# A plain first pair in every feed-forward stage, and weight sums made by accumulating DMAs

## The chip, the cores and the metric

One core of a Trainium2 chip runs the whole program. The time is the device time of one execution in microseconds (us). The engines are TensorE (PE in the profile, PEld for its weight loads), VectorE (DVE), ScalarE (ACT), GpSimd (POOL) and SyncE (SP), which issues the DMAs of the kernel before.

## What is computed

Two layers of an encoder on 512 tokens of 1024 channels, in float32. Each layer is a half-weighted feed-forward stage, a mixer (a gated spatial unit and a bidirectional mLSTM, with one input and one output projection), and a second half-weighted feed-forward stage; a root-mean-square norm stands ahead of each and at the end. Cut to the part that the change touches:

```python
def rms_norm(x, g):
    return x * lax.rsqrt(jnp.mean(x * x, axis=-1, keepdims=True) + EPS) * g

def swiglu(x, w_gate, w_up, w_down):
    return (jax.nn.silu(x @ w_gate) * (x @ w_up)) @ w_down

for l in range(DEPTH):
    h = x + 0.5 * swiglu(rms_norm(x, ffn1_norm[l]), ffn1_w_gate[l], ffn1_w_up[l], ffn1_w_down[l])
    h = h + mixer(rms_norm(h, mix_norm[l]))
    x = h + 0.5 * swiglu(rms_norm(h, ffn2_norm[l]), ffn2_w_gate[l], ffn2_w_up[l], ffn2_w_down[l])
return rms_norm(x, final_norm)
```

The hidden width of a feed-forward stage is 2816, which is 22 blocks of 128.

## The kernel before

Everything is kept transposed: 128 channels on the partitions, tokens along the row. A float32 operand is used as two rounded halves, hi and lo: ScalarE makes hi by a cast, VectorE makes lo by a subtraction, and each product is three matmuls (hi by hi, hi by lo, lo by hi) that accumulate in PSUM. The norm's gain is multiplied into the activations and its reciprocal root is multiplied into the result, so a product can begin before the statistics are known.

**Pairs.** There are four feed-forward stages. In each, the 22 hidden blocks of gate and up are made in 11 pairs (q = 0 to 10) of two blocks, in groups of 4, 4 and 3 pairs; behind each group stand 8 down products (line 206 to 208 on `pd`), which add to x. One pair computes gate and up for two blocks. As a two by two block product it is done in seven products by Strassen's method, in the form with shared sums (`strassen_pair`): the weights of the pair lie in DRAM as four blocks b11, b12, b22, b21 of 128x1024 (512 KB each), and the seven weight operands are b11, b12 - b11, b22 - that, b22, b12 - b22, b21 and b21 - the second sum. `pair_plan` makes them: four loads by SyncE and four subtractions on VectorE (`combine`, line 149), each followed by `halves` (cast at line 144, subtraction at line 145). The operands of the activations are A11, A12, A22 and four sums S1 to S4, for each of four pairs of channel blocks (j). `Wide.split` makes all seven as x comes in: A11, A12 and A22 are cast and split at lines 367 and 368, the four sums are formed at line 369 into `fb` and cast and split at lines 374 and 375. Each of the seven products is 24 matmuls of 256 columns (lines 159 to 161).

**The first stage's first pair** is done without Strassen, because x and the weights come in piece by piece: 16 products per j, from A11, A12, A22 and A21, of three matmuls of 256 columns each (lines 1060 to 1062), in four PSUM banks. `gated_plain` finishes it, with a reciprocal root over the full width (`rstd`, lines 325 to 341). In the other three stages the first pair is a Strassen pair with `opening` set: its first three products run over j = 0 to 2 together before they take j = 3, and the statistics come from `rstd_tok` and its `spread` within this pair.

**Buffers and order.** `take` hands out the weight operands in the order of the plan and has AHEAD of them made in advance (4 in a feed-forward stage). Halves alternate between two buffers of the phase (`whix`, `wlox`) and three shared ones (`whi`, `wlo`); down and mixer weights use the shared ones alone. Raw blocks alternate likewise between `rawx` (3) and `raw` (3). The framework's scheduler orders each engine's instructions at compile time by their place in the program and by when it expects their inputs and buffers; `issue_after` and `keep_in_program_order` pin a few.

Of the kernel before, what the change touches and what calls it, by code (L numbers as in the profile page):

```python
# [8 lines left out]
F32 = mybir.dt.float32  # L9
# [25 lines left out]
class Net:  # L35
    AHEAD = {"X": 4, "M": 2, "F": 2}
# [17 lines left out]
    def masks(self):  # L54
# [4 lines left out]
        make_identity(nc, self.ident)  # L59
        self.tri = []  # L60
# [63 lines left out]
    def rawx(self):  # L124
        self.turn += 1
        if self.turn % 2:
            return self.phase.tile([P, 1024], F32, tag="rawx", name="rawx", bufs=3)
        return self.wp.tile([P, 1024], F32, tag="raw", name="raw")

    def load(self, src):  # L130
        raw = self.rawx()
        self.nc.sync.dma_start(out=raw, in_=src.rearrange("p j i c -> p (j i c)"))
        return raw

# [47 lines left out]
    def load_parts(self):  # L182
        self.wturn = getattr(self, "wturn", 0) + 1
        raw = self.rawx()
# [156 lines left out]
A11, A12, A22, S3, S1, S2, S4 = range(7)  # L341


class Wide(Norm):
    def __init__(self, b, g):
        super().__init__(b, g)
        self.d = 0
        self.eng = b.nc.vector
        self.spread = None

    def split(self, x):
# [5 lines left out]
        if d % 2 == 0:  # L357
            self.fa = b.wide("fa").rearrange("p (q t) -> p q t", q=4)
            for q in (1, 0):
                nc.scalar.mul(self.fa[:, q, :], x[:, (1 - q) * 256:(2 - q) * 256], g)  # L360
            return
        fa = self.fa
# [3 lines left out]
        fb = b.wide("fb").rearrange("p (q t) -> p q t", q=4)  # L366
# [10 lines left out]
        self.last = fa  # L377
# [87 lines left out]
def strassen_pair(b, norm, rstd, opening):  # L465
# [3 lines left out]
    three = ((pa, A11), (pe, S1), (pb, S2))  # L469
    if opening:  # L470
        ws = [b.take() for _ in three]
        for js in (range(3), (3,)):
            for (p, idx), w in zip(three, ws):
                b.strassen(p, w, X, idx, True, js)
    else:
        for p, idx in three:
            b.strassen(p, b.take(), X, idx, True)
# [6 lines left out]
    spread = None  # L484
    if rstd is None:
        rstd, _, spread = norm.rstd_tok()
    b.strassen(pb, b.take(), X, S3, False)
    U = b.wide("U").rearrange("p (t i c) -> p t i c", t=2, i=2)
# [3 lines left out]
    nc.vector.tensor_tensor(out=U[:, 1], in0=q(pb), in1=q(e5), op=ALU.add)  # L492
    nc.vector.tensor_tensor(out=U[:, 0], in0=q(pe), in1=q(u2), op=ALU.add)
    b.strassen(pa, b.take(), X, A12, False)
    if spread is not None:
        spread()
# [6 lines left out]
    return halved(b, G, True), rstd  # L503


def pair_plan(blocks):
    st = {}

    def e0(b):
        st["b11"] = b.load(blocks[0])  # L510
        return b.halves(st["b11"])

    def e1(b):
        st["b12"] = b.load(blocks[1])
        b.combine(st["b11"], st["b12"], st["b11"])
        return b.halves(st["b11"])

    def e2(b):
# [653 lines left out]
```

## Time and profile before

| | |
|---|---|
| median of 3 runs | 1793.61 us (1792.57 to 1794.6) |
| the profiled execution | 1797.66 us |
| its span, first to last instruction | 1795.9 us |
| TensorE busy | 1759.7 us, 98% |
| VectorE busy | 1396.1 us, 78% |
| ScalarE busy | 868.7 us, 48% |
| GpSimd busy | 98.6 us, 5% |
| DMA moved | 173.60 MB, 97 GB/s on average |

The profile is one execution. The engines run side by side, so the shares do not add up. TensorE's matmuls overlap in their records, so its busy time is longer than the work at its pitch; how many matmuls of which width lie in a stretch tells more. The granted clock is the share of TensorE's full 2.4 GHz, 0.5 being 1.2 GHz. A wait is put down to what came last before it ended.

### The profile page before, as it was taken

How to read it: one execution, taken by the hardware profiler on the slowest of the kernel's cores; microseconds unless marked ns; L12 is line 12 of the kernel's file. 1: busy time of each engine (PE TensorE's matmuls, PEld its weight loads, DVE VectorE, ACT ScalarE, POOL GpSimd, SP SyncE). 2: the span in 40 equal slices, each digit the busy share in tenths (PEclk: the TensorE clock that was granted, in tenths of full speed). 3: DMA queues.
4: the chain of work that ended last, by engine and by line, in shares of the span. 5: the costliest groups of instructions: out<-in, count | busy, mean ns of one | idle time of the engine just before them, and what ended most of it. 6: DMA issues, size and time to landing. Idle time of an engine off the chain costs nothing.

```text
span 1795.9 us, 28343 instructions
## 1 busy us (share of the span) xinstructions
PE 1759.7 (98%) x11626; PEld 1610.3 (90%) x11626; DVE 1396.1 (78%) x2113; ACT 868.7 (48%) x1223; POOL 98.6 (5%) x164
## 2 busy tenths in 40 slices
PE   8999999999998999999989999999999999999998
PEld 8889989887888989989889899898888799899898
DVE  8967958667988957958889588595698989597685
ACT  7434424557555524525545244254576545254255
POOL 6100000103010000000010000002030000000000
PEclk9999999999998999999999999999999999999999
DMA  5332322321241333323323223223112224233223
GB/s 188 95 129 87 122 86 80 97 82 47 66 146 59 114 110 95 118 82 93 108 95 118 82 90 124 89 75 106 59 60 83 91 86 129 84 105 118 83 77 109
DMA packets 51394, 173.60 MB, mean 97 GB/s; under 512 B 5824, under 2 KB 7872, under 8 KB 51264
## 3 DMA queue, kind: packets, MB, share of 16 engines
q1 hardware_dynamic: 51264, 171.79, 29.9%
q8 instruction: 91, 1.49, 0.3%
q14 instruction: 39, 0.32, 0.1%
HBM read 169.67 MB, written 2.10 MB: 96 GB/s over the span
## 4 chain that ended last, share of the span: by engine, by line
PE 85%; DVE 9%; ACT 3%; issue 1%; DMA 1%; SPq 0%; POOL 0%; DVEq 0%; ACTq 0%; POOLq 0%
PE pd L206 9%; PE pd L208 9%; PE pd L207 9%; PE pb L159 6%; PE pb L160 6%; PE pb L161 6%; PE pe L160 4%; PE pa L159 4%; PE pa L160 4%; PE pe L159 4%; PE pa L161 4%; PE pe L161 4%; PE pm L206 3%; PE pm L207 3%; PE pm L208 3%
## 5 line engine op out<-in xcount | busy, mean ns | idle before, releaser
L179 ACT CAST whi<-raw 128x1024 fp32r<-128x1024 f32 (+2 forms) x157 | 151.9, 967 | 317.9 <-PE pd L207 157.5
L206 PE MATMUL pd<-hh,whi 128*128 128x512 f32 (+1 forms) x752 | 282.9, 377 | 0.4 <-ACT hh L448 0.4
L207 PE MATMUL pd<-hl,whi 128*128 128x512 f32 (+1 forms) x752 | 282.6, 376 | 0.6 <-DVE hl L449 0.6
L208 PE MATMUL pd<-hh,wlo 128*128 128x512 f32 (+1 forms) x752 | 282.6, 376 | 0.5 <-DVE wlo L180 0.5
L180 DVE TENSOR_TENSOR wlo<-raw,whi 128x1024 fp32r<-128x1024 f32 (+2 forms) x157 | 176.4, 1125 | 30.0 <-ACT whi L179 29.1
L598 DVE SCALAR_TENSOR_TENSOR x<-pd,x 128x512 f32<-128x512 f32 x88 | 60.7, 690 | 152.1 <-PE pd L208 152.0
L206 PEld LDWEIGHTS pd<-hh,whi 128*128 128x128 f32 x752 | 141.4, 188 | 29.5 <-ACT hh L448 4.3
L208 PEld LDWEIGHTS pd<-hh,wlo 128*128 128x128 f32 x752 | 141.6, 188 | 26.0 <-DVE wlo L180 0.8
L207 PEld LDWEIGHTS pd<-hl,whi 128*128 128x128 f32 x752 | 141.6, 188 | 26.0 <-DVE hl L449 0.8
L144 ACT CAST whi<-rawx 128x1024 fp32r<-128x1024 f32 x86 | 88.6, 1048 | 150.1 <-DVE rawx L149 92.0
L159 PE MATMUL pb<-xh,whix 128*128 128x256 f32 x528 | 153.2, 290 | 4.3 <-ACT u L482 3.4
L161 PE MATMUL pb<-xh,wlox 128*128 128x256 f32 x528 | 151.3, 287 | 0.6 <-DVE wlox L145 0.6
L160 PE MATMUL pb<-xl,whix 128*128 128x256 f32 x528 | 151.3, 286 | 0.0
L144 ACT CAST whix<-rawx 128x1024 fp32r<-128x1024 f32 x86 | 89.8, 1049 | 114.8 <-PE pb L160 80.1
L159 PE MATMUL pb<-xh,whi 128*128 128x256 f32 x504 | 142.2, 282 | 0.1
L160 PE MATMUL pb<-xl,whi 128*128 128x256 f32 x504 | 142.1, 282 | 0.0
L161 PE MATMUL pb<-xh,wlo 128*128 128x256 f32 x504 | 141.5, 281 | 0.5 <-DVE wlo L145 0.5
L144 ACT CAST whi<-raw 128x1024 fp32r<-128x1024 f32 x64 | 67.1, 1048 | 103.0 <-issue 40.5
L145 DVE TENSOR_TENSOR wlo<-rawx,whi 128x1024 fp32r<-128x1024 f32 x86 | 105.1, 1222 | 9.2 <-ACT whi L144 8.9
L145 DVE TENSOR_TENSOR wlox<-rawx,whix 128x1024 fp32r<-128x1024 f32 x86 | 105.0, 1221 | 9.1 <-ACT whix L144 9.1
L159 PEld LDWEIGHTS pb<-xh,whix 128*128 128x128 f32 x528 | 103.0, 195 | 5.8 <-ACT u L482 4.2
L159 PE MATMUL pe<-xh,whi 128*128 128x256 f32 x352 | 101.9, 290 | 5.4 <-ACT xh L374 5.4
(331 smaller groups left out, 5065.7 us busy)
## 6 DMA issues: line engine op xcount, KB each, us to landing
rawx<-in_wst SPq DMA_DIRECT2D x86, 512.0 KB, 3.6
raw<-in_wst SPq DMA_DIRECT2D x86, 512.0 KB, 3.6
raw<-in_wd SPq DMA_DIRECT2D x64, 512.0 KB, 3.6
raw<-in_wd SPq DMA_DIRECT2D x37, 384.0 KB, 3.1
raw<-in_win SPq DMA_DIRECT2D x24, 512.0 KB, 3.5
raw<-in_wo SPq DMA_DIRECT2D x16, 512.0 KB, 3.5
raw<-in_wv SPq DMA_DIRECT2D x8, 512.0 KB, 3.5
x<-in_xT SPq DMA_DIRECT2D x8, 256.0 KB, 4.0
```

The lines of the kernel that those rows point to most:

```text
L144: self.copied = nc.scalar.copy(hi, raw)
L145: nc.vector.tensor_tensor(out=lo, in0=raw, in1=hi.bitcast(F32), op=ALU.subtract)
L159: nc.tensor.matmul(o, whi[:, j, i, :], hi, start=f, stop=False, skip_group_check=True)
L160: nc.tensor.matmul(o, whi[:, j, i, :], lo, start=False, stop=False, skip_group_check=True)
L161: nc.tensor.matmul(o, wlo[:, j, i, :], hi, start=False, stop=j == 3, skip_group_check=True)
L179: self.copied = nc.scalar.copy(hi[:, r], raw[:, r])
L180: nc.vector.tensor_tensor(out=lo[:, r], in0=raw[:, r], in1=hi[:, r].bitcast(F32), op=ALU.subtract)
L206: nc.tensor.matmul(ps, whi[:, k0 + k, :], xh, start=k == 0, stop=False)
L207: nc.tensor.matmul(ps, whi[:, k0 + k, :], xl, start=False, stop=False)
L208: nc.tensor.matmul(ps, wlo[:, k0 + k, :], xh, start=False, stop=k == n - 1)
L598: nc.vector.scalar_tensor_tensor(out=xd, in0=pd, scalar=0.5, in1=xd, op0=ALU.mult, op1=ALU.add)
```

## The change

- Every feed-forward stage begins with a plain pair (`plain_plan`, `plain_step`), as the first stage did. Three Strassen pairs become plain ones.
- `Wide.split` makes A11, A12, A22 and A21 (hi and lo) only. `Wide.sums` makes the four sums for all j, in place, behind the plain pair's matmuls in the program; two of them with the opposite sign. The statistics come from `rstd_tok` behind it in all four stages. `spread` and `gated_plain` for the plain pair stand behind the first product (A11) of the second pair.
- The weight operands of a Strassen pair are made as running sums: p = b11, + b12, + b22, + b21 in one `rawx` tile, q = b22, + b12 in a `raw` tile, r = b21 in another. Each addition is a DMA issued by GpSimd that accumulates into the tile (`add`). The signs that differ are put right in the activations' sums and in two instructions of the pair's end, which become `scalar_tensor_tensor`. The `opening` form of the pair is gone.
- AHEAD in these stages is 5, the constants are made in two parts (`eye` earlier), and the ring for GpSimd's DMAs is 2048.

```diff
-    AHEAD = {"X": 4, "M": 2, "F": 2}
+    AHEAD = {"X": 5, "M": 2, "F": 2}
...
+    def add(self, raw, src):
+        self.nc.gpsimd.dma_start(out=raw, in_=src.rearrange("p j i c -> p (j i c)"), accum_op=ALU.add)
...
-    def combine(self, out, a, c):
-        self.nc.vector.tensor_tensor(out=out, in0=a, in1=c, op=ALU.subtract)
...
-A11, A12, A22, S3, S1, S2, S4 = range(7)
+A11, A12, A22, S3, S2, S4, S1 = range(7)
...
         nc.scalar.copy(hi[:, 0:3], fa[:, 1:4])
+        nc.scalar.copy(a21[:, 0], fa[:, 0])
         nc.vector.tensor_tensor(out=lo[:, 0:3], in0=fa[:, 1:4], in1=hi[:, 0:3].bitcast(F32), op=ALU.subtract)
-        sub = lambda o, a, c, op=ALU.subtract: nc.vector.tensor_tensor(out=fb[:, o - S3], in0=a, in1=c, op=op)
-        sub(S1, fa[:, 0], fa[:, 3], ALU.add)
-        sub(S2, fb[:, S1 - S3], fa[:, 1])
-        sub(S4, fa[:, 2], fb[:, S2 - S3])
-        sub(S3, fa[:, 1], fa[:, 0])
-        nc.scalar.copy(hi[:, 3:7], fb)
-        nc.vector.tensor_tensor(out=lo[:, 3:7], in0=fb, in1=hi[:, 3:7].bitcast(F32), op=ALU.subtract)
+        nc.vector.tensor_tensor(out=a21[:, 1], in0=fa[:, 0], in1=a21[:, 0].bitcast(F32), op=ALU.subtract)
...
+    def sums(self):
+        nc = self.b.nc
+        for fa, (hi, lo) in zip(self.fas, self.xs):
+            f = lambda i: fa[:, i - S3]
+            nc.vector.tensor_tensor(out=f(S1), in0=f(S1), in1=f(S3), op=ALU.subtract)
+            nc.vector.tensor_tensor(out=f(S3), in0=f(S2), in1=f(S3), op=ALU.subtract)
+            for o, a, m in ((S2, f(S1), f(S2)), (S4, f(S4), f(S2))):
+                nc.vector.scalar_tensor_tensor(out=f(o), in0=a, scalar=-1.0, in1=m, op0=ALU.mult, op1=ALU.subtract)
+            nc.scalar.copy(hi[:, 3:7], fa)
+            nc.vector.tensor_tensor(out=lo[:, 3:7], in0=fa, in1=hi[:, 3:7].bitcast(F32), op=ALU.subtract)
...
+    def whole(name, src, chain):
+        def make(b):
+            st[name] = b.load(src, chain)
+            return b.halves(st[name])
+        return make
+
+    def more(name, src):
+        def make(b):
+            b.add(st[name], src)
+            return b.halves(st[name])
+        return make
+
+    return [whole("p", b11, True), more("p", b12), more("p", b22), whole("q", b22, False), more("q", b12),
+            whole("r", b21, False), more("p", b21)]
+
+
+def plain_plan(blocks):
+    def whole(k):
+        return lambda b: b.halves(b.load(blocks[k], k % 2 == 0))
+    return [whole(k) for k in range(4)]
...
+            if q == 0:
+                banks = first
+                if banks is None:
+                    blocks = [b.take() for _ in range(4)]
+                    banks = plain_banks(b)
+                    for j in range(4):
+                        plain_step(b, norm, j, blocks, banks)
+                norm.sums()
+                rstd["full"], _, spread = norm.rstd_tok()
+
+                def between():
+                    spread()
+                    hs.extend(gated_plain(b, *banks, rstd["full"]))
+
                 continue
-            h, rstd = strassen_pair(b, norm, rstd, q == 0)
-            hs += h
+            hs.extend(strassen_pair(b, norm, lambda: rstd["full"], between if q == 1 else None))
```

## Rows read from the trace of the kernel before

**Rows 1.** The page's first lines: span, busy time and instructions of TensorE.

```profile
span 1795.9 us, 28343 instructions
PE 1759.7 (98%) x11626; PEld 1610.3 (90%) x11626; DVE 1396.1 (78%) x2113; ACT 868.7 (48%) x1223; POOL 98.6 (5%) x164
```

**Rows 2.** Windows: stretch, length, busy us (x instructions), PEclk, DMA share, GB/s.

```profile
40.00:80.00 40.00, 34.17 (x251) 32.89 (x251) 36.94 (x38) 17.86 (x21) 11.05 (x22) 0.91 0.30 89
180.00:200.00 20.00, 20.00 (x171) 20.00 (x170) 18.90 (x20) 9.55 (x11) 0.00 (x0) 1.00 0.33 95
240.00:260.00 20.00, 20.00 (x90) 16.58 (x89) 7.67 (x8) 4.10 (x4) 0.00 (x0) 1.00 0.32 99
545.00:581.00 36.00, 30.69 (x209) 28.73 (x208) 31.22 (x52) 17.44 (x25) 0.00 (x0) 0.86 0.19 60
901.00:937.00 36.00, 31.35 (x226) 29.41 (x225) 30.72 (x51) 15.93 (x20) 6.93 (x19) 0.91 0.35 108
1428.00:1464.00 36.00, 30.67 (x207) 28.77 (x206) 30.66 (x50) 17.04 (x25) 0.00 (x0) 0.86 0.20 59
```

**Rows 3.** TensorE's waits in 540:580: us, times, longest.

```profile
PE pe L159 <- ACT xh L374: 2.6, 2, 2.0
PE pe L160 <- DVE xl L375: 0.9, 1, 0.9
PE pa L160 <- DVE xl L368: 0.9, 1, 0.9
PE pa L159 <- ACT xh L367: 0.9, 1, 0.9
```

**Rows 4.** VectorE's groups of instructions in 525:575: count, busy us, mean ns, idle.

```profile
L979 DVE TENSOR_TENSOR x<-pm,x 128x512 f32<-128x512 f32 x8 | 5.4, 682 | 0.6 <-PE pm L208 0.6
L375 DVE TENSOR_TENSOR xl<-fb,xh 128x1024 fp32r<-128x1024 f32 x4 | 4.9, 1220 | 0.0
L368 DVE TENSOR_TENSOR xl<-fa,xh 128x768 fp32r<-128x768 f32 x4 | 3.8, 949 | 0.0
L369 DVE TENSOR_TENSOR fb<-fa 128x256 f32<-128x256 f32 x8 | 3.3, 434 | 0.0
```

**Rows 5.** ScalarE's timeline, 160:171: start, us, instruction, idle before and releaser.

```profile
160.51 1.05 ACT L144 CAST whix<-rawx 128x1024 fp32r<-128x1024 f32 x1 [0.58 <-PE pe L160]
164.17 2.00 ACT L144 CAST whi<-rawx 128x1024 fp32r<-128x1024 f32 x2 [2.61 <-DVE rawx L149]
169.99 1.05 ACT L144 CAST whix<-rawx 128x1024 fp32r<-128x1024 f32 x1
```

**Rows 6.** TensorE's timeline: first matmul of three successive products of one pair.

```profile
168.91 0.28 PE L159 MATMUL pa<-xh,whix 128*128 128x256 f32 x1
171.78 0.28 PE L159 MATMUL pe<-xh,whi 128*128 128x256 f32 x1
...
174.61 0.28 PE L159 MATMUL pb<-xh,whix 128*128 128x256 f32 x1
```

**Rows 7.** VectorE's timeline, 161:171: the split of a block, and a sum of blocks.

```profile
161.59 1.23 DVE L145 TENSOR_TENSOR wlox<-rawx,whix 128x1024 fp32r<-128x1024 f32 x1 [0.26 <-ACT whix L144]
162.85 1.22 DVE L149 TENSOR_TENSOR rawx<-raw,rawx 128x1024 f32<-128x1024 f32 x1
```

**Rows 8.** The page's DMA issues: count, KB each, median us from issue to landing.

```profile
rawx<-in_wst SPq DMA_DIRECT2D x86, 512.0 KB, 3.6
...
raw<-in_wd SPq DMA_DIRECT2D x37, 384.0 KB, 3.1
```

**Rows 9.** GpSimd's timeline, 0:100: two equal products of the parameters.

```profile
33.96 1.30 POOL L660 TENSOR_TENSOR rv<-rv,ct 128x64 f32<-128x64 f32 x1
...
39.14 0.32 POOL L660 TENSOR_TENSOR rv<-rv,ct 128x64 f32<-128x64 f32 x1
```

**Rows 10.** The chain's long pieces, and TensorE's timeline where one product starts within another.

```profile
39.02 3.27 DVE rstd L336
...
82.54 0.28 PE L160 MATMUL pa<-xl,whix 128*128 128x256 f32 x1
82.66 0.39 PE L159 MATMUL pb<-xh,whi 128*128 128x256 f32 x1
```

More of the change, by code (lines that the diff above doesn't have):

```diff
@@ L122, in take, with load @@
         return self.ready.pop(0)
[L124 to L131, printed above, removed]
+    def load(self, src, chain=False):
+        raw = (self.phase.tile([P, 1024], F32, tag="rawx", name="rawx", bufs=3) if chain else
+               self.wp.tile([P, 1024], F32, tag="raw", name="raw"))
         self.nc.sync.dma_start(out=raw, in_=src.rearrange("p j i c -> p (j i c)"))
         return raw
+    def add(self, raw, src):
+        self.nc.gpsimd.dma_start(out=raw, in_=src.rearrange("p j i c -> p (j i c)"), accum_op=ALU.add)
     def halves(self, raw):
@@ L462, in gated_plain, with plain_banks, plain_step, strassen_pair @@
     return halved(b, g)
-def strassen_pair(b, norm, rstd, opening):
+def plain_banks(b):
+    return [b.bank("mm", "pm") for _ in range(2)], [b.bank("sm", "pm") for _ in range(2)]
+def plain_step(b, norm, j, blocks, banks):
+    nc = b.nc
+    pg, pu = banks
+    hi, lo = norm.xs[j]
+    for k, out, second in ((0, pg, False), (1, pu, False), (3, pg, True), (2, pu, True)):
+        whi, wlo = blocks[k]
+        for i in range(2):
+            for th in range(2):
+                o = out[i][:, th * 256:(th + 1) * 256]
+                if not second and th:
+                    xh, xl = norm.low[j]
+                else:
+                    idx = (A22 if th else A12) if second else A11
+                    xh, xl = hi[:, idx, :], lo[:, idx, :]
+                f = j == 0 and not second and th == 0
+                nc.tensor.matmul(o, whi[:, j, i, :], xh, start=f, stop=False, skip_group_check=True)
+                nc.tensor.matmul(o, whi[:, j, i, :], xl, start=False, stop=False, skip_group_check=True)
+                nc.tensor.matmul(o, wlo[:, j, i, :], xh, start=False, stop=second and j == 3, skip_group_check=True)
+def strassen_pair(b, norm, get, between=None):
     nc = b.nc
@@ L468, in strassen_pair @@
     pa, pe, pb = b.bank("mm", "pa"), b.bank("sm", "pe"), b.bank("mm", "pb")
[L469 to L477, printed above, removed]
+    b.strassen(pa, b.take(), X, A11, True)
+    if between is not None:
+        between()
+    b.strassen(pe, b.take(), X, S1, True)
+    b.strassen(pb, b.take(), X, S2, True)
     s1, e5, u2 = (b.slot(name=n) for n in ("s1", "e5", "u2"))
@@ L483, in strassen_pair @@
     b.strassen(pe, b.take(), X, S4, False)
[L484 to L486 removed]
     b.strassen(pb, b.take(), X, S3, False)
+    rstd = get()
     U = b.wide("U").rearrange("p (t i c) -> p t i c", t=2, i=2)
@@ L547, in ffn_plan @@
         for q in range(m0 // 2, (m0 + nk) // 2):
-            if q > 0 or not first:
-                yield from pair_plan([wst[q, k] for k in range(4)])
+            blocks = [wst[q, k] for k in range(4)]
+            if q > 0:
+                yield from pair_plan(blocks)
+            elif not first:
+                yield from plain_plan(blocks)
         for d in range(ND):
@@ L1036, in trunk_kernel @@
     raws = [b.load_parts() for _ in range(4)]
-    pg, pu = [b.bank("mm", "pm") for _ in range(2)], [b.bank("sm", "pm") for _ in range(2)]
+    blocks = [tuple(t.rearrange("p (j i c) -> p j i c", j=4, i=2) for t in r[1:]) for r in raws]
+    banks = plain_banks(b)
     for j in range(4):
@@ L1041, in trunk_kernel @@
             cur.split(x[:, d, :])
-        a21 = b.slot(F32R, name="a21").rearrange("p (k t) -> p k t", k=2)
-        nc.scalar.copy(a21[:, 0, :], cur.last[:, 0, :])
-        nc.vector.tensor_tensor(out=a21[:, 1, :], in0=cur.last[:, 0, :], in1=a21[:, 0, :].bitcast(F32), op=ALU.subtract)
-        hi, lo = cur.xs[j]
         for k in range(4):
             b.fill((wst[0, 0, k].rearrange("p j i c -> p (j i c)"), *raws[k]), j * 256, (j + 1) * 256)
-        for k, banks in ((0, pg), (1, pu), (3, pg), (2, pu)):
-            s = k in (2, 3)
-            whi, wlo = (t.rearrange("p (j i c) -> p j i c", j=4, i=2) for t in raws[k][1:])
-            for i in range(2):
-                for th in range(2):
-                    o = banks[i][:, th * 256:(th + 1) * 256]
-                    if not s and th:
-                        xh, xl = a21[:, 0, :], a21[:, 1, :]
-                    else:
-                        idx = (A22 if th else A12) if s else A11
-                        xh, xl = hi[:, idx, :], lo[:, idx, :]
-                    f = j == 0 and not s and th == 0
-                    nc.tensor.matmul(o, whi[:, j, i, :], xh, start=f, stop=False, skip_group_check=True)
-                    nc.tensor.matmul(o, whi[:, j, i, :], xl, start=False, stop=False, skip_group_check=True)
-                    nc.tensor.matmul(o, wlo[:, j, i, :], xh, start=False, stop=s and j == 3, skip_group_check=True)
+        plain_step(b, cur, j, blocks, banks)
+    b.eye()
     held = {}
```

62 lines of the change are left out of this document (20 added, 42 removed).

## The prediction, made before the change was run

> **What bounds the kernel now.** I read the page's totals first: TensorE is busy for 98% of a span of 1795.9 us [rows 1]. A busy share of pipelined matmuls does not say that they run at their pitch, so the second view is the count of matmuls in stretches [rows 2]. Where a group of pairs runs undisturbed, 20 us hold 171 matmuls of 256 columns, 0.117 us each; where the down products run, 90 of 512 columns, 0.222 us each. These are the floors. VectorE is busy for 18.9 of the 20 us there and still TensorE is never late: in the steady part the limit is TensorE, and taking work from VectorE buys nothing there. The openings are different. Four stretches hold fewer matmuls than fit: 40:80 has 251 (29.4 us of work, 10.6 lost), 545:581 has 209 (24.5 of 36, 11.5 lost), 901:937 has 226 (26.4, 9.6 lost), 1428:1464 has 207 (24.2, 11.8 lost). The granted clock falls to 0.86 to 0.91 of full on average there (part of the time at 1.2 instead of 2.4 GHz), which these losses contain. What ends the waits in one of them is a cast or a subtraction of activations (L367, L368, L374, L375) [rows 3]: TensorE waits for the split and the seven operands that the first product of a pair needs at once, and VectorE does these behind its residual adds.
>
> Terms are made against the profiled execution, 1797.7 us; its median sibling is 1793.6, so 4.1 is taken off at the end.
>
> **The change, part by part.**
>
> *The plain first pair.* It takes four weight blocks and 16 products of 256 columns, three matmuls each, in each of four steps: 192 matmuls against 7 x 24 = 168. The first stage has one already; three stages get 24 more: 3 x 24 x 0.117 = 8.4 us on the path.
> What it gives: step j needs only the split of its own two rows of x (x adds, one cast and subtraction of 768 elements, a small one for A21). Step 0 can run when the last output product ends, and steps 0 to 2 are 3 x 48 x 0.117 = 16.8 us of cover for the last split, a chain of an add, casts and a subtraction of under 1 us each [rows 4]. So I cost the three openings at none: -32.9 us.
> The sums move behind it: per step four of 0.43 us and a subtraction of 1.22 [rows 4], 2.9 us, 11.8 in all, and the statistics. With two blocks' subtractions they make some 17 us of VectorE in the 22.5 us that the plain pair takes, and the next pair's first product (2.8 us, which needs A11 alone) stands ahead of the first sum that is used. If the cover is gone, up to 3 us come back per stage.
>
> *The first stage.* Its plain pair exists. The full-width reciprocal root goes (one of its instructions takes 3.27 us [rows 10]), a narrow one comes, and the gating is put behind the next pair's first product. VectorE was full there and loses four combinations of 1.2 us per pair. Between nothing and all of the 10.6 us can be won; its start also depends on the weights, below, so I take half, -5.3.
>
> *The sums of weight blocks by DMA.* Removed: four VectorE subtractions of 1.22 us per pair [rows 7], in 43 pairs. In the steady part that is worth nothing (above). Added: four accumulating DMAs per pair issued by GpSimd in place of one load and those four. Each waits for the cast and the subtraction that read the tile before, and the next cast waits for its landing. On SyncE's queue there are three loads per pair instead of four; on GpSimd the adds queue behind each other and, in the first and third stage, behind the parameters' small products, of which a next one is at most 1.3 us away [rows 9].
> Price L of one add, from VectorE's last read to landing: no row shows a DMA of GpSimd or one that accumulates. Below, the same 512 KB plain, from SyncE: 3.6 us. Another 128 KB cost 0.5 us [rows 8], so reading the tile's 512 KB as well adds 2.0: 5.6. Above, GpSimd's part as long as its longest small product, 1.3: 6.9. I take 5.6, as the add reads both operands.
> By the Trainium skill (DMA: Bandwidth & Descriptors, Anatomy of one DMA — SWDGE (gpsimd) path) a DMA of GpSimd takes about 2.0 us plus its bytes at 436 GB/s; for twice 512 KB that would be an estimate of 4.4 us, at which the stalls below vanish and the sum would be some 1764 us. No row here shows such a DMA.
>
> How much of L shows: blocks' halves alternate between two whix and three whi buffers, so a block in whix is cast when the one three products earlier has been used. The trace has it: cast at 160.51 ended by TensorE [rows 5], used at 168.91 [rows 6], 8.4 us ahead, its subtraction done at 162.82 [rows 7], 6.1 ahead. Products follow at 2.85 us. Now take a pair whose first block sits in whix, time 0 at its first product. First subtraction ends at -6.1; first sum lands L later, is cast and split in 2.3; the second lands another L later, split in 2.3: ready at 2L - 1.5, used at 5.7. It is late by 2L - 7.2, 4.0 us at 5.6. Two other products of the pair (A12 with the plain block b21, S4 with plain b22) need none of it, 5.7 us. Does the compiler's schedule put them ahead? It does such things already: two whi casts in a row at 164.17 [rows 5] mean that b22's overtook the second sum's, and the product at 82.66 starts in the midst of another [rows 10]. So the loss is 2L - 12.9, none up to L = 6.45. A pair whose first block is in whi starts up to three products earlier and is safe.
> The first pair of each stage is worse. The plain pair holds both whix buffers until its last step; the first is free 36 matmuls (4.2 us) before the end, so the first subtraction ends at -1.9. First sum ready at L + 0.4 = 6.0, with 5.7 us to fill: 0.3 lost. Second sum ready at 2L + 2.7 = 13.9, with 6.0 + 5.7 filled: 2.2 lost. That is 2.5 per stage, 10 in four.
>
> One block more of lead in the plan (the buffers set the lead, above), the split of the constants, the signs (the same count of VectorE instructions) and the larger ring cost nothing that a row could show.
>
> **Sum.** -32.9 + 8.4 - 5.3 + 10 = -19.8: 1777.9, and less 4.1 for the median, 1774.
>
> **The rivals.**
> *The adds are slow.* Decides against the change from L = 6.8: 16 pairs (every second one, without the first) lose 2L - 12.9 and the four first pairs 2L - 8.7 together 40L - 241, which at 6.8 eats the 29.8 that the rest gives. For it: GpSimd and doubled reads are unmeasured; three loads and four adds share 16 DMA engines that are a third busy now [rows 2]. At L = 8: +49, 1843 us. Chance 0.25.
> *The schedule keeps the products' order.* Then at 5.6 the 16 pairs lose 4.0, the first pairs 8.2, eight pairs behind down products about 1.5: 109 - 29.8 = +79, 1873. Against it: rows 5 and 10. Chance 0.08.
> *VectorE holds GpSimd up.* Of GpSimd's equal products one takes 1.30 us and one, 5 us later, 0.32 [rows 9], and VectorE is busy nearly all the time about there [rows 2]. If issuing an add suffers so each time, L = 6.9: 40L - 241 = 35, net +5, 1798 or, nearly as likely, a few us less: no change. The Trainium skill (SBUF — State Buffer, Who interferes with whom) says that a VectorE instruction with two SBUF inputs holds up GpSimd instructions that read SBUF, and that a 2-port mode also holds up the writing of descriptors; the two durations agree with the first, and no run here shows the second. Chance 0.07.
> *The openings are only half cured*, because VectorE is still behind when the sums are needed (3 us per stage and half of the clock's share): -5 to 0, about 1790. Chance 0.05.
>
> **How the numbers follow.** The forecast, 1774, has 0.55; its own range runs from 1758 (L = 3.6, all of the first stage's loss won: -32.9 - 10.6 + 8.4 = -35.1) to 1789. The range reaches up to L = 8, 1845, and leaves out the kept order and longer adds. About 0.2% is what a measurement of this kernel can tell from no change. Faster 0.56 (forecast and a little of the half cure), same 0.09, slower 0.35.
>
> **What would show it.** Right: 192 matmuls at full pitch behind each last output product, at 0.117 us and full clock; no wait for L374 and L375 there; VectorE about 14 of 20 us in the pairs; POOL-issued adds that land 5 to 6 us after VectorE's read; plain blocks' products ahead of the second sum's in every second pair. Wrong: TensorE's waits ended by casts of rawx after a DMA, each 1 to 5 us, in every second pair and above all in the first; adds landing after 7 us or more; or VectorE still ending TensorE's waits at the openings.

## The result, and the profile after

The changed kernel takes 2048.70 us (median; 2042.64 to 2050.33), the kernel before 1793.14 us beside it. The ratio is 1.1418, with a 95% interval of 1.1393 to 1.1443: 14% slower. The forecast was 1774 us, with a range up to 1845.

First the page's totals of the changed kernel, its row of granted clock, GpSimd's DMA queue (packets, MB, share of 16 engines), and what its DMA issues cost (count, KB each, median us from issue to landing):

```profile
span 2048.2 us, 28819 instructions
PE 1850.2 (90%) x11706; PEld 1678.9 (82%) x11706; DVE 1200.8 (59%) x1948; ACT 851.8 (42%) x1215; POOL 221.1 (11%) x324
PEclk8999998999999998999998999989999989999999
q0 software_dynamic: 23040, 83.90, 25.1%
...
rawx<-in_wst POOLq DMA_DIRECT2D x120, 512.0 KB, 5.6
raw<-in_wst SPq DMA_DIRECT2D x86, 512.0 KB, 3.9
...
raw<-in_wst POOLq DMA_DIRECT2D x40, 512.0 KB, 8.3
```

TensorE, busy for 98% before [rows 1], is at 90%; VectorE fell from 78% to 59% and nobody gains by it. The adds into p's tile land 5.6 us after their issue, the price that the forecast took; the adds into q's tile take 8.3. The next two views say where TensorE stands: windows (stretch, length, busy us and instructions of each engine, PEclk, DMA share, GB/s) of a plain pair and of the first 20 us behind a group of down products, and TensorE's waits over the whole span (us, times, longest).

```profile
608.00:630.00 22.00, 22.00 (x189) 22.00 (x187) 11.83 (x20) 7.16 (x10) 1.06 (x1) 1.00 0.04 3
164.50:184.50 20.00, 13.70 (x93) 13.05 (x93) 7.29 (x8) 5.64 (x7) 2.60 (x3) 0.84 0.69 158
```

```profile
PE pb L157 <- ACT whix L145: 58.6, 16, 5.2
PE pe L157 <- ACT e L507: 53.5, 29, 6.0
PE pb L157 <- ACT whi L145: 14.7, 12, 2.2
PE pb L157 <- ACT u L509: 14.5, 17, 2.1
PE pa L157 <- ACT s L506: 11.8, 3, 4.1
PE pb L159 <- DVE wlo L146: 10.2, 14, 0.8
PE pb L159 <- DVE wlox L146: 9.2, 16, 0.8
```

The plain pair is all that was promised: 189 matmuls in 22 us at full clock, where the opening before had 209 in 36 us [rows 2]. The pairs are not. In the second stretch 93 matmuls stand where an undisturbed pair has 171 [rows 2], and the clock is 0.84. The waits fall into two kinds: for casts and splits of weights (lines 145 and 146), and for the copies s1, e5 and u2 that empty a PSUM bank (lines 506 to 509).

For the comparisons below I use one measure, worked out from the trace: the time from the start of one matmul to the start of the next, less the 0.119 us that 256 columns take in an undisturbed stretch (0.227 for 512), summed. I call it TensorE's lost time. It is 69.0 us before and 311.0 after, and 283 of the 311 lie in the 40 Strassen pairs. Of the 311, steps of more than 0.15 us over the pitch make 233 (117 for casts and splits of weights, 89 for the copies, 27 for the rest); the other 78 are matmuls that run below their pitch behind such a wait (22 before).

One such place in order of time, from the timelines of TensorE, VectorE, GpSimd and ScalarE (start, us, instruction, idle before and releaser; the pair that begins at 164.55 in the window above), and below them two windows, one of the wait and one behind it:

```profile
167.39 0.28 PE L157 MATMUL pe<-xh,whix 128*128 128x256 f32 x1
...
171.42 0.38 PE L157 MATMUL pb<-xh,whi 128*128 128x256 f32 x1 [1.00 <-ACT whi L145]
...
180.09 0.58 PE L157 MATMUL pe<-xh,whix 128*128 128x256 f32 x1 [4.54 <-ACT e L507]
```

```profile
154.73 1.22 DVE L146 TENSOR_TENSOR wlo<-rawx,whi 128x1024 fp32r<-128x1024 f32 x1 [0.16 <-ACT whi L145]
163.32 1.22 DVE L146 TENSOR_TENSOR wlox<-rawx,whix 128x1024 fp32r<-128x1024 f32 x1 [3.31 <-ACT whix L145]
...
171.40 1.23 DVE L146 TENSOR_TENSOR wlo<-rawx,whi 128x1024 fp32r<-128x1024 f32 x1 [5.12 <-ACT whi L145]
```

```profile
156.31 0.86 POOL L134 DMA_DIRECT2D rawx<-in_wst  x1 [51.28 <-DVE wlo L146]
164.90 0.86 POOL L134 DMA_DIRECT2D rawx<-in_wst  x1 [7.73 <-DVE wlox L146]
166.17 0.86 POOL L134 DMA_DIRECT2D raw<-in_wst  x1 [0.41 <-issue]
172.99 0.87 POOL L134 DMA_DIRECT2D rawx<-in_wst  x1 [5.95 <-DVE wlo L146]
```

```profile
153.65 1.05 ACT L145 CAST whi<-rawx 128x1024 fp32r<-128x1024 f32 x1 [4.39 <-PE pd L206]
162.24 1.05 ACT L145 CAST whix<-rawx 128x1024 fp32r<-128x1024 f32 x1 [7.54 <-DMA rawx<-in_wst]
163.19 1.05 ACT L145 CAST whix<-raw 128x1024 fp32r<-128x1024 f32 x1
170.33 1.04 ACT L145 CAST whi<-rawx 128x1024 fp32r<-128x1024 f32 x1 [6.09 <-PE pe L158]
173.60 1.05 ACT L145 CAST whi<-raw 128x1024 fp32r<-128x1024 f32 x1 [2.23 <-DMA raw<-in_wst]
174.56 0.58 ACT L506 COPY s<-pa 128x512 f32<-128x512 f32 x1
175.03 1.05 ACT L145 CAST whix<-raw 128x1024 fp32r<-128x1024 f32 x1
178.50 1.04 ACT L145 CAST whi<-rawx 128x1024 fp32r<-128x1024 f32 x1 [2.42 <-DMA rawx<-in_wst]
179.46 0.58 ACT L507 COPY e<-pe 128x512 f32<-128x512 f32 x1
```

```profile
175.60:180.05 4.45, 0.00 (x0) 0.00 (x0) 2.01 (x3) 2.02 (x3) 0.00 (x0) 0.79 0.98 261
180.05:185.40 5.35, 5.31 (x26) 5.31 (x27) 1.37 (x2) 0.64 (x2) 0.00 (x0) 0.54 0.40 150
```

Read them as one chain, all of it on p's tile. b11 is cast at 153.65, when a down product has freed a whi buffer. The first add is issued when VectorE has read the tile (156.31) and the sum is cast at 162.24. VectorE's read of it ends at 164.54, the second add is issued at 164.90, its sum cast at 170.33; read until 172.63, third add at 172.99, its sum cast at 178.50. Each link is some 8 us: the add, 5.7 to 6.3 us from the end of VectorE's read to landing (155.95 to 162.22, 164.54 to 170.23, 172.63 to 178.48, by the trace's landing times), and the 2.3 us of cast and subtraction. (The profile puts the wait of the cast at 170.33 down to a matmul that ended 0.07 us after the landing.) TensorE asks for a link every 2.9 us. The order of its products is the program's: pa, pe, pb, pe, pb, pa, pb. By the starts of all matmuls it is so in 36 of the 40 pairs; in the four behind plain pairs some of A12's matmuls run ahead of the second sum's product (S2), and S4 is ahead of it in none.

And there is a second effect. The third sum is needed only by the pair's last product, but its cast stands on ScalarE's queue ahead of e5. The product behind pe ended at 170.42; its copy e5 is made at 179.46, behind a cast that waited for a DMA until 178.48, and the fourth product (S4), whose operand b22 was long there, starts at 180.09. Behind that wait TensorE runs at 0.54 of its clock, near the lower of its two levels: 26 matmuls in 5.35 us in place of 3.1.

### The profile page after: what moved, and what is told of

Its sections match the earlier page's. It is cut to its first block, busy times and chain, and to the rows that moved or that the text cites. A ratio compares the mean times of both kernels' runs of the same rounds, so it can differ in the third digit from the quotient of the medians.

```text
span 2048.2 us, 28819 instructions
## 1 busy us (share of the span) xinstructions
PE 1850.2 (90%) x11706; PEld 1678.9 (82%) x11706; DVE 1200.8 (59%) x1948; ACT 851.8 (42%) x1215; POOL 221.1 (11%) x324
## 3 DMA queue, kind: packets, MB, share of 16 engines
q0 software_dynamic: 23040, 83.90, 25.1%
## 5 line engine op out<-in xcount | busy, mean ns | idle before, releaser
L134 POOL DMA_DIRECT2D rawx<-in_wst x120 | 104.5, 871 | 1353.0 <-DVE wlo L146 703.9
L145 ACT CAST whi<-rawx 128x1024 fp32r<-128x1024 f32 x80 | 83.7, 1046 | 316.1 <-DMA rawx<-in_wst 258.7
L157 PE MATMUL pb<-xh,whix 128*128 128x256 f32 x480 | 153.9, 321 | 63.2 <-ACT whix L145 58.6
L146 DVE TENSOR_TENSOR wlo<-rawx,whi 128x1024 fp32r<-128x1024 f32 x80 | 98.0, 1225 | 168.1 <-ACT whi L145 168.1
L178 DVE TENSOR_TENSOR wlo<-raw,whi 128x1024 fp32r<-128x1024 f32 (+2 forms) x157 | 176.6, 1125 | 30.7 <-ACT whi L177 29.8
L157 PE MATMUL pe<-xh,whix 128*128 128x256 f32 x320 | 100.2, 313 | 43.3 <-ACT e L507 43.3
L158 PE MATMUL pb<-xl,whi 128*128 128x256 f32 x480 | 137.9, 287 | 0.0
```

The costliest lines, as they stand in the source:

```text
L134: self.nc.gpsimd.dma_start(out=raw, in_=src.rearrange("p j i c -> p (j i c)"), accum_op=ALU.add)
L145: self.copied = nc.scalar.copy(hi, raw)
L146: nc.vector.tensor_tensor(out=lo, in0=raw, in1=hi.bitcast(F32), op=ALU.subtract)
L157: nc.tensor.matmul(o, whi[:, j, i, :], hi, start=f, stop=False, skip_group_check=True)
L158: nc.tensor.matmul(o, whi[:, j, i, :], lo, start=False, stop=False, skip_group_check=True)
L178: nc.vector.tensor_tensor(out=lo[:, r], in0=raw[:, r], in1=hi[:, r].bitcast(F32), op=ALU.subtract)
```

## The experiments

Theory A: each add costs what the forecast said, and the loss is the length of the chain cast, subtraction, add, cast against the lead that the buffers give, since the order of the products is kept. The rivals stand with the runs. Kernels without an interval below ran for a single execution (the adds alone for two); the kernel before lay between 1789.5 and 1796.4 us beside them. The four executions of the changed kernel spread over 7.7 us, so a few us between two of these kernels mean nothing.

| kernel | us | lost time | its waits: weights / copies |
|---|---|---|---|
| before | 1793 | 69 | 6 / 6 |
| changed | 2049 | 311 | 117 / 89 |
| plain opening alone | 1790 | 52 | 18 / 6 |
| adds alone | 1997 | 264 | 105 / 61 |
| adds replaced by SyncE's loads | 1804 | 66 | 11 / 17 |
| adds replaced by GpSimd's plain DMAs | 1843 | 104 | 32 / 33 |
| copies on VectorE | 2056 | 317 | 92 / 105 |
| alternation shifted | 1950 | 211 | 77 / 61 |
| own tiles for two sums | 1881 | 142 | 42 / 50 |
| last cast pinned | 1997 | 258 | 139 / 16 |
| lead of 3 alone | 2027 | 288 | 108 / 78 |
| A12 early | 1998 | 260 | 71 / 82 |
| whix blocks first (no adds) | 1789 | 50 | 18 / 6 |
| next pair starts in whi (no adds) | 1781 | 43 | 15 / 1 |

**Which half of the change costs.** Two kernels, each with one half; the first also has the lead (AHEAD) of 4 and the alternation of raw blocks of the kernel before.

```diff
 # plain opening alone, against the changed kernel
-            b.add(st[name], src)
+    def combine(self, out, a, c):
+        self.nc.vector.tensor_tensor(out=out, in0=a, in1=c, op=ALU.add)
...
 # adds alone: the kernel before with pair_plan, load, add of the changed one, its signs, AHEAD 5 and ring
```

> The change without its accumulating DMAs: each stage begins with the plain pair and makes the activation sums behind it, but the four sums of weight blocks are VectorE additions again, as before. Theory A (the whole loss comes from the adds, the plain opening does what the forecast said): the openings' 32.9 us less 8.4 for 72 more matmuls, and about half of the first stage's 10.6, so 1762 to 1772 us. Rival B (the plain pair itself costs: it holds both whix buffers to its end, and the sums behind it make VectorE late in the pairs that follow): above 1800 us, with TensorE waits in the first pair of each stage on L368-like sums.

> The kernel before with nothing changed but the sums of weight blocks: they are made by accumulating DMAs (signs adapted, one block more of lead, the larger ring). Theory A: the pairs of a group lose about 7 us each as in the changed kernel, 43 pairs, so 2050 to 2110 us. Rival B (adds and plain opening hurt each other: the loss needs the plain pair that holds the buffers): only the pairs behind a plain pair suffer, below 1900 us here.

The plain opening alone takes 1789.56 us, ratio 0.9979 (0.997 to 0.9987): 3 us less than before. The adds alone take 1997 us, 205 more. So the loss comes from the adds, and it does not need the plain pair. But theory A missed both kernels: the first lies some 20 us above its range, the second 53 us below it (and 97 above rival B's), and adds on top of the plain opening cost 259 us (2049 less 1790), not 205.

Where the opening's gain went is read from its windows: the plain pair with what leads up to it, and the pair behind it. Two lines of ScalarE's and VectorE's timelines follow.

```profile
545.00:567.00 22.00, 22.00 (x189) 22.00 (x187) 13.95 (x22) 8.06 (x11) 0.00 (x0) 1.00 0.01 1
567.00:593.00 26.00, 22.39 (x178) 21.30 (x177) 24.01 (x38) 12.06 (x14) 0.00 (x0) 1.00 0.24 82
```

```profile
562.15 1.05 ACT L147 CAST whix<-rawx 128x1024 fp32r<-128x1024 f32 x1 [7.57 <-PE pm L496]
```

```profile
563.24 1.23 DVE L148 TENSOR_TENSOR wlox<-rawx,whix 128x1024 fp32r<-128x1024 f32 x1 [7.21 <-ACT whix L147]
```

The plain pair is at full pitch; the next 26 us hold 178 matmuls where 222 fit. The first block's cast waited 7.6 us for the plain pair to free a whix buffer, VectorE stood idle for 7.2 us, and then it had everything at once (24 of 26 us busy). The four openings lost 40.1 us before (10.0, 11.0, 7.8, 11.3). Now the three new plain pairs lose nothing, and the pairs behind the four plain ones 27.6 (10.6, 4.7, 6.1, 6.2): 12.5 us won, and 72 more matmuls take 8.6 of it (72 x 0.119).

**What one step costs.** In two kernels each add became a plain DMA of the same block into the same tile, so that all waits stay.

```diff
-        self.nc.gpsimd.dma_start(out=raw, in_=src.rearrange("p j i c -> p (j i c)"), accum_op=ALU.add)
+        self.nc.sync.dma_start(out=raw, in_=src.rearrange("p j i c -> p (j i c)"))      # one kernel
+        self.nc.gpsimd.dma_start(out=raw, in_=src.rearrange("p j i c -> p (j i c)"))    # the other
```

> The changed kernel with each accumulating DMA replaced by a plain load of the same block into the same tile from SyncE's queue; the sums are left out, so the output differs. Every wait stays: the load still waits for the cast and the subtraction that read the tile. Only the price of the step falls, from 5.6 us (8.3 for the sum in q's tile) to about 3.6 to 4.0. Theory A (the price of the step, multiplied along the chain): at 2L - 7.2 the second sum is late by 0 to 0.8 us, so nearly all of the loss goes: 1770 to 1830 us. Rival C (the chain of waits is too long at any price, because the order of TensorE and ScalarE is fixed): still above 1900 us. A load that waits also holds back the loads behind it on SyncE's queue, which can add some loss under either.

> The changed kernel with each accumulating DMA replaced by a plain one from GpSimd's queue; the sums are left out, so the output differs. It tells what GpSimd's issue costs and what accumulating costs. If the second operand's bytes are the price (the forecast's 2.0 us of the 5.6), the DMAs land 3.6 to 4.4 us after their issue and the time falls to 1780 to 1870 us. If GpSimd's path itself is slow, they land after 5 us or more and the time stays above 1950 us.

From SyncE: 1804 us. From GpSimd: 1843 us, within what was expected if accumulating is the price. The issues of the kernel with SyncE's loads (here the first loads of the tiles are counted in), then of the one with GpSimd's:

```profile
rawx<-in_wst SPq DMA_DIRECT2D x166, 512.0 KB, 3.7
raw<-in_wst SPq DMA_DIRECT2D x126, 512.0 KB, 3.9
```

```profile
rawx<-in_wst POOLq DMA_DIRECT2D x120, 512.0 KB, 3.9
...
raw<-in_wst POOLq DMA_DIRECT2D x40, 512.0 KB, 4.9
```

The 160 loads of the changed line alone land after 3.6 us (p's tile) and 4.4 (q's) from SyncE, by their landing times in the trace. So GpSimd's path costs 0.3 us more than SyncE's for p's tile, accumulating another 1.7. The time follows the price: a pair's three steps into p and one into q sum to 15.2 us (3 x 3.6 + 4.4), 16.6 (3 x 3.9 + 4.9) and 25.1 (3 x 5.6 + 8.3). Over 40 pairs these are 608, 664 and 1004 us, and the lost time is 66, 104 and 311: 0.68 us for each further microsecond in the first step, 0.61 in the second. With SyncE's price the chain nearly fits, some 15 us above the plain opening alone. This is theory A; rival C, too long at any price, is out.

**What a link less is worth.** The first sum and the sum in q's place get tiles of their own, into which the plain block is loaded once more, so that these adds wait for a load only.

```diff
-    return [whole("p", b11, True), more("p", b12), more("p", b22), whole("q", b22, False), more("q", b12),
+    return [whole("p0", b11, False), own("p", b11, b12), more("p", b22), whole("q", b22, False), own("q1", b22, b12),
...
```

> The changed kernel, but the first sum of a pair and the one in q's place are made in tiles of their own (the plain block is loaded a second time there, and the DMA adds to it), so that these two adds wait for a load and not for the cast and the subtraction of the block before. The outputs are the same; two loads of 512 KB per pair come on top. Theory A (price of an add times the length of the chain cast, subtraction, add, cast): one of three links of the chain is gone and q's altogether; the second sum would be ready 0.5 us before its use at 6.1 us from read to landing, so most of the 283 us that the pairs lose go: 1790 to 1840 us. Rival G (adds are slow because GpSimd's path and the DMA engines are loaded, whatever waits for them): with more traffic they land later still, and the time stays above 1950 us.

1881 us: 168 us less with as many adds and two loads more per pair, but 41 above what theory A gave, and 69 below rival G's. The adds now land after 7.0 us in place of 5.6.

```profile
rawx<-in_wst POOLq DMA_DIRECT2D x160, 512.0 KB, 7.0
```

More than the loads, it is the adds that hold each other up: the 48 of them that overlap no other add landed after 5.6 us (median), as 34 such did in the changed kernel (5.7), and the 79 that share over 4 us with another after 8.0 (55 and 7.0 in the changed kernel). Loads count as well: beside 90 to 140 GB/s of them a lone add took 6.5 us (11 adds). So the length of the chain carries most of the loss, and the price of a link grows with what runs beside it. A single wait of 17.1 us in the first stage's first pair is 15% of what these pairs still lose; what caused it was not followed up.

**Which buffer a pair begins in.** By kind of pair, the changed kernel loses: the four pairs behind plain ones 43.8 us, the eight behind down products (beginning in whi) 75.6, the other sixteen that begin in whix 122.9, the other twelve in whi 40.8. In the kernel with the adds alone the alternation falls otherwise; in its second and fourth stage the pairs behind down products begin in whix, and they lose nothing. So the alternation was shifted:

```diff
+            if q in (3, 10):
+                yield None          # take: self.wturn += 1, no block
```

> The changed kernel with one thing shifted: behind the fourth and the eleventh pair of a stage the alternation of the buffers skips one turn, so that the pairs directly behind down products begin in a whix buffer, not in a whi one that the down products' units hold. Theory E (what a pair loses is set by the kind of buffer that its blocks fall into): in the kernel with the adds alone pairs behind down products that begin in whix lose nothing, other whix pairs 6 to 8 us and whi pairs 2 to 3, against 9.3 us for the changed kernel's pairs behind down products. By these the seven pairs of the two later groups lose 22 us in place of 47 in each stage, four stages, so 1950 us (1930 to 1975). Rival F (pairs behind down products lose whatever buffer they begin in, by what the down products leave on the queues): 2030 to 2065 us.

1949.87 us. The eight pairs behind down products fall from 75.6 us to nothing; the first 20 us of the pair whose chain is shown above are undisturbed:

```profile
164.60:184.60 20.00, 20.00 (x169) 19.95 (x169) 10.64 (x11) 6.71 (x8) 2.42 (x3) 1.00 0.68 154
```

The cause is in the timeline above: a block in whi can only be cast when a down product frees the buffer (153.65, 11 us ahead of the pair), while whix is idle during down products. That these pairs lose nothing at the same DMA share (0.68 against 0.69 in the stretch) shows that their losses come from the lead and not from traffic.

**ScalarE's queue.** Three kernels on the copies that stand behind casts.

```diff
 # copies on VectorE
-    nc.scalar.copy(s1, pa)
-    nc.scalar.copy(e5, pe)
+    nc.vector.tensor_copy(s1, pa)
+    nc.vector.tensor_copy(e5, pe)
-    nc.scalar.copy(u2, pb)
+    nc.vector.tensor_copy(u2, pb)
 # last cast pinned
-    AHEAD = {"X": 5, "M": 2, "F": 2}
+    AHEAD = {"X": 3, "M": 2, "F": 2}
+        if pin:                               # only for the block p + b21
+            self.tc.keep_in_program_order(self.copied)
 # lead of 3 alone: only the AHEAD line
```

> The changed kernel with the three evacuation copies of a pair (s1, e5, u2) made by VectorE instead of ScalarE. Theory D (a good part of the loss is ScalarE's queue: the copies stand behind weight casts that wait for an accumulating DMA to land, and TensorE waits for the copies): TensorE's waits on L506, L507 and L509, 12.2 + 58.9 + 17.9 = 89 us and their share of half-clock time, fall to under a third, 1940 to 1990 us. Rival A' (the copies are only what shows last; the sums that are late are needed just as soon): the same time is waited for whix and whi casts instead, above 2010 us.

> The changed kernel with the cast of a pair's last sum pinned on ScalarE's queue behind the three evacuation copies of its pair (and two blocks less of lead in the plan, so that it is written behind them). Theory D' (the order on ScalarE's queue is what costs: the compiler puts the last sum's cast ahead of e5 and u2, as it counts on an earlier landing, and the copies then wait for a DMA that nobody needs yet): the waits on L507 and L509, 58.9 + 17.9 us, go and a part of the half-clock time with them, 1930 to 1990 us. Rival A' (the chain of adds is late as a whole, and what is taken from one wait is found in the next): 2020 us or more.

> The changed kernel with two blocks less of lead in the plan (3 in place of 5) and nothing else: the other half of the pinned kernel, which came to 1996.8 us. If the pin on ScalarE's queue did that, this one stays at 2035 to 2060 us; if the shorter lead did it, by another order of the compiler's, it comes to 1985 to 2010 us, and the pin showed nothing.

Moved to VectorE the copies gain nothing, 2056 us: they now wait behind subtractions, which wait for the same casts, and the waits for them went from 89 to 105 us. Pinned behind the copies, the last cast no longer holds them: their waits fell from 89 to 16 us, and the time to 1997. But the shorter lead alone gives 2027, so 22 us belong to the lead and 30 to the pin. Both lie between what the theories expected. In the pinned kernel the same pair reads:

```profile
155.68 1.05 ACT L145 CAST whi<-rawx 128x1024 fp32r<-128x1024 f32 x1 [4.39 <-PE pd L208]
...
177.24 0.59 ACT L509 COPY e<-pe 128x512 f32<-128x512 f32 x1
...
182.78 1.05 ACT L145 CAST whi<-rawx 128x1024 fp32r<-128x1024 f32 x1 [2.54 <-DMA rawx<-in_wst]
```

Counted from the pair's first cast (155.68 there, 153.65 above), e5 comes 4.3 us earlier and the last sum's cast 2.3 us later. The waits for casts and splits grew from 117 to 139 us. The queue's order is a cause of its own, but it is worth some 30 us here, not the 89 that are put down to the copies: most of that was the late sums, seen at another place.

**The order of the products.** What the forecast expected of the compiler, done by hand:

```diff
     b.strassen(pe, b.take(), X, S1, True)
+    b.strassen(pa, b.take(), X, A12, False)
     b.strassen(pb, b.take(), X, S2, True)
 # and r = b21 behind p + b12 in pair_plan
```

> The changed kernel with the product of the plain block b21 (A12) moved, in the plan and in the program, from behind the sum in q to ahead of the second sum's product (S2): the move that the forecast expected of the compiler. Theory A (the second sum is late by a fixed time, 2L - 7.2 or 5 us at 6.1 us from read to landing): 2.85 us more until it is used, in 40 pairs, so up to 114 us less, of which up to 1.2 us per pair are given back because A22's product now follows S3's in the same bank: 1930 to 1990 us. Rival J (the sum in q and the last sum are what is late): no gain, 2030 us or more.

1998 us, 50 less, just above theory A's range. But the move did not take place in the pairs that it was meant for: in the sixteen that begin in whix behind another pair the compiler put the first two of S2's matmuls ahead of A12's, so TensorE waits for the second sum before it comes to A12. One such place in TensorE's timeline, and its waits over the whole span:

```profile
200.97 0.58 PE L157 MATMUL pb<-xh,whi 128*128 128x256 f32 x1 [4.93 <-ACT whi L145]
...
202.40 0.58 PE L157 MATMUL pa<-xh,whix 128*128 128x256 f32 x1 [0.64 <-ACT s L505]
```

```profile
PE pb L157 <- ACT whi L145: 66.0, 16, 4.9
PE pa L157 <- ACT s L505: 46.5, 34, 12.8
...
PE pb L157 <- DVE U L518: 11.0, 9, 3.1
```

The 66.0 us are those sixteen waits for the second sum (58.6 in the changed kernel; its block falls into whi here), and the sixteen pairs lose 132.7 us in place of 122.9. In the twenty pairs that begin in whi, A12 does run first, and they lose 46.9 us in place of 116.4 (29.4 behind down products, 17.5 the others). The other waits are new: A12 accumulates into the bank that s1 must have been copied from, and A22 follows S3 in the bank that line 518 reads. So where the order changed, some 3.5 us per pair were won, about what theory A has (2.85 and the clock behind a wait), though this kernel also moves sums to other buffers. For the sixteen pairs that the forecast's formula is about, the other order remains untested.

**The opening's own loss.** Two kernels without adds.

```diff
 # whix blocks first: in the plain pair's last step
+    for k, out, second in (ks[0], ks[3], ks[1], ks[2]) if j == 3 else ks:
 # next pair starts in whi: besides, one turn of the alternation skipped behind each plain pair, and one ahead of the next
```

> The kernel with the plain opening and VectorE's sums of weight blocks, and the four blocks of the plain pair's last step in another order: the second whix block directly behind the first, so that both whix buffers come free 24 matmuls (2.8 us) earlier or more. The first pairs behind a plain pair lose 4.7, 6.1 and 6.2 us there, 11.0 of it for whix casts. Theory H (the first sums are late because the plain pair holds the whix buffers to its end): half or more of the 17 us goes, 1777 to 1784 us. Rival I (VectorE's activation sums and weight sums set the pace of the first pair): no change, 1787 to 1791 us.

> The kernel with the plain opening, VectorE's sums and the plain pair's last step with its whix blocks first, and the alternation shifted by one behind the plain pair, so that the first block of the next pair goes into the third whi buffer, which is free, and not into a whix buffer that the plain pair holds. In the kernel without the shift VectorE stood idle for 7.2 us ahead of the first pair, until that first block was cast. Theory H' (the first pair is late by the time that its first cast waits for a whix buffer): the 4.6 to 4.8 us of the three later first pairs and some of the 10.5 of the first stage go, 1768 to 1780 us. Rival I (VectorE's activation sums and weight sums are too much for the first pair wherever they begin): 1785 to 1791 us.

The first changes little against the plain opening alone: 1788.63 us, ratio to before 0.9975 (0.9966 to 0.9984), where that one had 0.9979. This is rival I's range; but the first whix buffer comes free no earlier in this kernel (its cast still waits 7.6 us for the plain pair), and the chain begins there, so it tested little. With the first block in the free whi buffer the pairs behind the three later plain pairs lose 2.5, 1.3 and 2.5 us, the first stage's still 9.4, and the time is 1781.10 us, ratio 0.9940 (0.9928 to 0.9952): 1 us above theory H', 4 below rival I. The same stretch as above:

```profile
544.00:566.00 22.00, 22.00 (x188) 22.00 (x187) 17.29 (x26) 10.02 (x14) 0.00 (x0) 1.00 0.01 1
566.00:592.00 26.00, 24.03 (x194) 22.99 (x193) 22.45 (x37) 13.24 (x15) 0.00 (x0) 1.00 0.26 82
```

VectorE works 17.3 us ahead of the pair in place of 14.0, and the next 26 us hold 194 matmuls, not 178. It is the fastest kernel here, without accumulating DMAs.

## Why the prediction was wrong, point by point

The forecast put the loss of all Strassen pairs at 10 us, in the four behind plain pairs. It is 283: 43.8 in those four, 122.9 in the sixteen that begin in whix behind another pair, 75.6 in the eight behind down products, 40.8 in the other twelve that begin in whi. The steps, in the forecast's order:

**What bounds the kernel: right.** Taking 4 x 1.22 us per pair from VectorE bought nothing in the steady part.

**The price of an add: right for p, wrong for q.** 5.6 us from bounds of 3.6 and 6.9; measured 5.6 from issue and 5.7 to 6.3 from VectorE's last read. The sum in q's tile costs 8.3: all 40 of its adds are issued while one into p's tile is under way, 28 of them 1.0 to 1.3 us behind it. The forecast had no term for that. The rival that VectorE holds GpSimd up does not show: the 120 issues of adds into p take nearly the same time.

```profile
L134 POOL DMA_DIRECT2D rawx<-in_wst x120: 853/862/1177, 39.4 to 1982.7; - x120
```

(shortest, median and longest in ns.) The slow-adds rival put its break-even at 6.8 us and was not needed: 5.6 was already too much.

**"Does the compiler's schedule put them ahead?": this is the step that failed.** The forecast took it that A12 and S4 would be put ahead of the second sum's product, and with that set the loss to 2L - 12.9, none up to 6.45 us. The two places that it took for this do not show it. The casts of [rows 5] changed places on ScalarE's queue, but the products for which they were made stand in the program's order, pa, pe, pb [rows 6]; and the product at 82.66 [rows 10] is a pair's last one, which starts within the first of the next pair. By the starts of all matmuls, in none of the 43 Strassen pairs of the kernel before does A12 or S4 begin ahead of the second sum's product. In the changed kernel A12 does in part in the four pairs behind plain ones, S4 in none. Then the forecast's own other formula, 2L - 7.2, holds: none at 3.6, and with SyncE's loads at 3.6 these waits are all but gone; 4.0 at 5.6 us and 5.0 at 6.1, and 4.2 was measured (58.6 and 9.2 us for whix casts and splits, in 16 pairs). The sixteen pairs lose 7.7 each (122.9 / 16), of which 5.8 are waits and the rest matmuls at the lower clock. The rival that described this had a chance of 0.08. Why the compiler keeps the order is not shown. The adds are not needed for it: with plain loads in their place, and with VectorE's sums, neither A12 nor S4 begins ahead of the second sum's product in these pairs.

**That rival was too small too**: 109 us (64 + 33 + 12) for its three kinds of pairs, where they lose 242 (123, 44, 76), and the twelve whi pairs 41. It lacked the clock behind a wait, the late sum in q's tile, and the rest below.

**"A pair whose first block is in whi ... is safe": wrong.** Behind down products it is the worst of the steady pairs, 9.4 us each (75.6 / 8, against 1.5), since down products use the whi buffers; the shift of the alternation takes all of it away. The forecast had taken whi's lead from a place inside a group.

**"One block more of lead ... cost nothing": not so.** With a lead of 3 in place of 5 the changed kernel takes 22 us less, mostly in the four pairs behind plain ones (22.5 us lost in place of 43.8). A lead of 4 with adds was not run.

**Instructions behind the waiting one.** The forecast named what waits for an add (the next cast) and not what stands behind that cast on ScalarE's queue: three copies that TensorE needs sooner. This shows as 89 us of waits; what the order itself costs is about 30.

**The openings: the mechanism right, the size wrong.** Plain pairs run at full pitch, but the sum of -32.9, -5.3 and +8.4 us is -29.8, and measured it is -3. The term that was mis-sized is -32.9: the three later openings lost 30.1 us before, and the pairs behind the plain ones lose 17.0 of it again. "The plain pair holds both whix buffers until its last step" stood in the text and was counted only against adds; VectorE's sums start just as late by it. With the first block moved to the free whi buffer it is -10 (1791.56 to 1781.10). In the first stage nothing was won (10.0 us lost before, 10.6 now).

**The clock** was counted only as a gain at the openings. It falls behind waits: 78 us of the lost time in the changed kernel are matmuls below pitch.

## What to carry to other kernels

When a step moves from an engine to a DMA that must wait for the readers of its own tile, count the links of the chain and set them against the lead that the buffers give at the worst place (behind a stage that holds the same buffers), at the order in the program. A compiler's reordering is a hope until it has been seen on the queue that matters: casts that change places on ScalarE say nothing of products on TensorE. An engine that is not the limit need not be relieved: here a subtraction of 1.22 us in the shadow became a transfer of 6 us in a chain. A change with two halves should be priced and run as two: one half was worth 10 us once its own stall was found, the other cost 200 and more.

## What the runs showed of the hardware

- Accumulating into SBUF cost 1.7 us in a DMA of 512 KB, on top of a plain one of the same queue (5.6 against 3.9). By the Trainium skill (DMA: Bandwidth & Descriptors, Anatomy of one DMA — SWDGE (gpsimd) path) the estimate in the forecast was 4.4 us, 1.2 less than was measured, and for a plain one the page's fit gives an estimate of 3.2 us where 3.9 was measured; the measurements decide.
- GpSimd is busy 0.87 us to issue one accumulating DMA and 0.54 for a plain one (POOL's groups of 120 at line 134: 104.5 and 64.3 us). The same 23040 packets and 83.90 MB occupied 25.1% of 16 engines' 2048 us in the changed kernel, and 14.3% of 1842 in the plain one: 0.36 and 0.18 us per packet, twice as long.
- Two accumulating DMAs issued 1.27 us apart landed after 5.33 and 7.33 us. Where the add into p's tile and the one into q's were under way together (40 times), the first took 5.5 us and the second 8.3 (medians).
- Behind a wait of 4.5 us TensorE ran below full clock: 0.54 granted in the next 5.35 us, 26 matmuls where 45 fit at the pitch.
